# A two-layer streaming encoder on one core: pooling mixer by halves of 512 columns, its bands and cached tokens parked in DRAM ahead, and running sums of log f formed with the projections

## The chip, the cores and the metric

One core of one Trainium2 chip runs the whole program as a single launch. The metric is device time in microseconds (us). Engines are called PE (TensorE), DVE (VectorE), ACT (ScalarE), POOL (GpSimd) and SP (SyncE); SP issues nearly all of this kernel's DMAs, in the order in which they stand in its queue. All data are float32 at the interface. Every large product is made from three single-pass products of a high and a low part (`hi`, `lo`, `xh`, `xl`, `uh`, `ul`): `hi` is the rounded copy (`fp32r`) and `lo` the rest.

## What is computed

One inference step of two layers over 1,152 tokens: 1,024 of a new prompt, and 16 new tokens of each of 8 running streams. Model width 1,024, feed-forward width 2,816.

- Layer 0's mixer: one projection gives q, f, i, g of a gated linear recurrence (HGRN, 4 heads of 128) and q, k, v of a differential attention (4 heads), which runs over the prompt and over 2,048 cached tokens of each stream; an output projection follows.
- Layer 1's mixer pools the last 2, 4, 8 or 16 rows per group of 256 channels, with 15 cached rows for each stream, and multiplies each group by its 256x256 weight.
- Each mixer is followed by a layer norm, a feed-forward block with a convolution over three rows (ConvFFN), and a layer norm.

The recurrence, and the pooling, which the change touches:

```python
def hgrn2_chunk(S0, q, log_f, k, v):
    b = jnp.cumsum(log_f, axis=1)
    decay = jnp.where(causal, jnp.exp(jnp.minimum(b[:, :, None] - b[:, None, :], 0.0)), 0.0)
    scores = jnp.einsum('bthk,btshk,bshk->bhts', q, decay, k)
    o = einsum('bhts,bshv->bthv', scores, v) + einsum('bthk,bhkv->bthv', q * jnp.exp(b), S0)
    S = S0 * jnp.exp(b[:, -1])[..., None] + einsum('bshk,bshv->bhkv', k * jnp.exp(b[:, -1:] - b), v)

def mixer_pool(x, pos0, hist, w_groups, scale):
    xh = jnp.concatenate([hist, x], axis=1)
    cs = jnp.cumsum(jnp.pad(xh, ((0, 0), (1, 0), (0, 0))), axis=1)
    for g, w in enumerate((2, 4, 8, 16)):
        s = cs[:, 16:, sl] - cs[:, 16 - w:16 - w + T, sl]
        outs.append((s / minimum(w, pos + 1) - x[..., sl]) @ w_groups[g])
    return jnp.concatenate(outs, axis=-1) * scale, xh[:, -15:]
```

## The kernel before

The tokens are nine tiles of 128 rows: tiles 0 to 7 the prompt, tile 8 the streams (`NPT = 8`, `NT = 9`). A tile framework reorders instructions over the engines by priority, and gives buffers by tag; an instruction that writes into a tag whose buffers are all in use waits until one is free. The stages around the change, in the order of the program:

1. **Projections.** `fm_group` (L369) makes q, k and log f for each of the four heads with features on partitions, 128 x 1,152, and stores them to the DRAM scratch `fm_scr` (`out_fm`, L385). The last DVE step for log f is the subtraction at L401; its store stands in SP's queue among the loads `kraw` and `vraw` of cached keys and values. This stage is woven with the attention of the streams over their cached tokens.
2. **HGRN** (`hgrn`, L803). Nine blocks of 128 tokens in two lanes: the stream block (8), 1, 3, 5, 7 and 0, 2, 4, 6. For m = 1, 2, 4, ..., 64 (four levels for the stream block) `level_prep` makes one level: with tokens in pairs of runs of m, `qk` holds q times the decay from the pair's middle in the second run, and k times the decay up to it in the first. Two running tiles are kept for this, `P` (sums of log f from the start of a run to the token) and `sf` (from the token to the run's end). Each level ends with DVE adding a run's total onto the next one, in place, for `sf` (L847) and `P` (L849), on half of the 512 columns; the first level copies and clears `sf` (L842, L843). So the next level's exponentials (ACT) come after this level's sums. `put` multiplies `qk` on PE and copies the scores under a mask (L861, L873). When all levels are through, `edge_prep` makes `qb` and `kb` (L894, L895) for the state's part, and `outputs` or `outputs_streams` the products with v and the state S. Attention of the remaining streams is woven in, and gives PE other work.
3. **ConvFFN of layer 0.** The second product runs by groups of two of the 22 feature blocks; a group is nine tiles of twelve matmuls `pd`, and DVE adds each into `acc` (L1471). Weights come through `raw` (3 buffers) and are cast into `wh`, `wl` (8 buffers each), a group ahead.
4. **Pooling mixer** (`pool_mixer`, L1575). At its start SP loads two thirds of the window matrices (`band`, 128 x 128 for each term and channel group) into `raw` and DVE casts them (L1553). For each tile n, `project` multiplies the tile by the scaled pool weights into PSUM `pu` (24 matmuls of 256 columns) and splits it into `uh`, `ul` (128 x 1,024, 3 buffers each); `windows(n-1)` applies the band matrices to tiles n-1 and n-2 (`py`, 16 matmuls), adds into `acc` (L278), and starts the layer norm; `to_xt` transposes an older tile (`pxt`) for the next block. At n = 4, `bring_history` loads the 120 cached rows (`hist`), transposes them (`ph`, 8 on PE), splits them into `hh`, `hl`, and the last two band matrices are loaded and cast.

```python
            for n in range(NT + 1):
                if n == 4:
                    bring_history()
                    band_s = load_bands(pw, 3, 2)
```

Helpers: L144 issues a matmul, L153 a transpose, L156/L157 the split into a high part (ACT) and a low part (DVE or POOL), L278 the residual addition, L243 to L249 the layer norm's last steps.

Of the kernel before, what the change touches and what calls it, by code (L numbers as in the profile page):

```python
# [111 lines left out]
def hybrid_stream_kernel(ctx: ExitStack, tc: tile.TileContext, i, o, k):  # L112
# [198 lines left out]
    t4_scr = [dr.tile([4, 2, 128, NTOK // 2], F32, name=f"t4_scr{l}") for l in range(2)]  # L311
    g_scr = [dr.tile([NF, 128, NTOK], F32, name=f"g_scr{l}") for l in range(2)]
# [56 lines left out]
    def fm_group(st, c0, which):  # L369
        wh, wl = load_cols(w_in, c0)  # L370
        for j in range(2):
# [29 lines left out]
            nc.vector.tensor_tensor(lf, z, lf, ALU.subtract)  # L401
            out_fm(lf, 1)
# [397 lines left out]
    def hgrn(hg, hc, fm0, v0, before_last):  # L800
# [13 lines left out]
        def begin(bi):  # L814
# [10 lines left out]
            blk[bi] = dict(q=fm[0], P=fm[1], k=fm[2], v=v, sf=sf, sc=sc)  # L825

        def level_prep(bi, mi):
            B = blk[bi]
            q, P, kf, sf = B["q"], B["P"], B["k"], B["sf"]
            m = LEVELS[mi]  # L830
            g = 512 // (2 * m)
# [51 lines left out]
        def edge_prep(bi):  # L883
# [4 lines left out]
            nc.scalar.activation(kb, B["sf"], AF.Exp)  # L888
# [549 lines left out]
    def ffn_down(l, last, ahead):  # L1438
# [108 lines left out]
    def load_bands(pool, j0, n):  # L1547
        band = pool.tile([128, n, 4, 128], F32R, name=f"band{j0}")
        for j in range(0, n, 2):
            m = min(2, n - j)  # L1550
# [22 lines left out]
    def pool_mixer(acc, late, ws):  # L1573

        with ExitStack() as ph:  # L1575
            pw = pool_of(ph, "wpl", 1)
            band = load_bands(pw, 0, 3)
# [10 lines left out]
            def bring_history():  # L1588
                hist = raw_tile("hist")
                nc.sync.dma_start(hist[0:120, :], i["state_pool"][0].rearrange("b j d -> (b j) d"))  # L1590
                for j in range(0, KD, 4):
                    p = bank([128, 4, 120], "ph")
                    for q in range(4):
                        tr(p[:, q, :], hist[0:120, (j + q) * 128:(j + q + 1) * 128], 120)
                    split(hh[:, j:j + 4], hl[:, j:j + 4], p)

            def project(fh, fl, n):
                uh = sp.tile([n, D], F32R, tag="uh", name="uh", bufs=3)
                ul = sp.tile([n, D], F32R, tag="ul", name="ul", bufs=3)
                for j in range(2):  # L1600
                    p = bank([n, 2, 256], "pu")
                    for gg in range(2):
# [101 lines left out]
```

## Time and profile before

| | us |
|---|---|
| three timed runs | 2553.20, 2555.87, 2557.08 (median 2555.87) |
| the profiled execution | 2553.18 |
| its span, first to last instruction | 2551.2 |
| PE busy | 2487.2 (97%) |
| DVE, ACT, POOL busy | 1509.5 (59%), 1069.5 (42%), 954.6 (37%) |
| mean granted clock of PE | 0.988 of full speed |

Times in the trace count from the span's start. "Busy" is the time in which an engine has an instruction in hand. A list of waits names, for each engine, the line that waited and the line or DMA that released it. A table by stretch gives busy time for each engine between two points, with the clock granted to PE, as a fraction of 2.4 GHz. Stages by time: projections with cached-token attention up to about 585, HGRN from there to about 760, the first ConvFFN up to about 1660, the pooling mixer from about 1640 to 1762, the second ConvFFN after it.

### The profile page before, as it was taken

How to read it: one execution, taken by the hardware profiler on the slowest of the kernel's cores; microseconds unless marked ns; L12 is line 12 of the kernel's file. 1: busy time of each engine (PE TensorE's matmuls, PEld its weight loads, DVE VectorE, ACT ScalarE, POOL GpSimd, SP SyncE). 2: the span in 40 equal slices, each digit the busy share in tenths (PEclk: the TensorE clock that was granted, in tenths of full speed). 3: DMA queues.
4: the chain of work that ended last, by engine and by line, in shares of the span. 5: the costliest groups of instructions: out<-in, count | busy, mean ns of one | idle time of the engine just before them, and what ended most of it. 6: DMA issues, size and time to landing. Idle time of an engine off the chain costs nothing.

```text
span 2551.2 us, 45246 instructions
## 1 busy us (share of the span) xinstructions
PE 2487.2 (97%) x18042; PEld 2305.0 (90%) x18042; DVE 1509.5 (59%) x2652; ACT 1069.5 (42%) x2167; POOL 954.6 (37%) x726
## 2 busy tenths in 40 slices
PE   8999999998999999999999999969999999999998
PEld 8999998886879999999999788869999999987886
DVE  3377754348984484555555655777655555556557
ACT  3255555354772544444444121266344444431114
POOL 1110111006642555555554122244455555531214
PEclk9999999998999999999999999989999999999999
DMA  5634337787866214222224322223232222252222
GB/s 181 193 107 132 95 129 244 241 268 240 255 200 243 98 55 148 78 78 70 71 78 172 125 97 80 78 62 108 98 115 78 78 70 70 78 210 96 84 92 84
DMA packets 279250, 323.78 MB, mean 127 GB/s; under 512 B 46347, under 2 KB 209748, under 8 KB 279039
## 3 DMA queue, kind: packets, MB, share of 16 engines
q1 hardware_dynamic: 276613, 319.26, 38.6%
q8 instruction: 142, 2.33, 0.4%
q10 hardware_dynamic: 2426, 1.63, 0.3%
q14 instruction: 69, 0.57, 0.1%
HBM read 244.38 MB, written 76.46 MB: 126 GB/s over the span
## 4 chain that ended last, share of the span: by engine, by line
PE 64%; DVE 2%; ACT 2%; issue 1%; DMA 1%; POOL 0%; DVEq 0%; SPq 0%; ACTq 0%; POOLq 0%
PE pu L144 39%; PE pd L144 20%; PE po L144 4%; DVE acc L243 1%; PE pxt L153 1%; ACT junk_ln L237 1%; ACT acc L244 0%; DMA graw<-g_scr 0%; DVE xl L157 0%; DVE acc L278 0%; DVE gl L157 0%; DMA raw<-in_ffn_w_up 0%; DMA hist<-in_state_pool 0%; PE pc L153 0%; POOL acc L249 0%
## 5 line engine op out<-in xcount | busy, mean ns | idle before, releaser
L157 POOL TENSOR_TENSOR lo<-raw,hi 128x512 fp32r<-128x512 f32 x360 | 514.6, 1443 | 1086.7 <-ACT hi L156 963.8
L144 PE MATMUL pu<-xl,hi 128*128 128x288 f32 (+1 forms) x1536 | 469.6, 306 | 2.8 <-DVE xl L157 2.8
L144 PE MATMUL pu<-xh,hi 128*128 128x288 f32 (+1 forms) x1536 | 470.4, 306 | 0.0
L144 PE MATMUL pu<-xh,lo 128*128 128x288 f32 (+1 forms) x1536 | 469.6, 306 | 0.0
L156 ACT CAST hi<-raw 128x512 fp32r<-128x512 f32 x376 | 229.0, 620 | 530.3 <-PE pu L144 263.3
L144 PE MATMUL pd<-lo,gh 128*128 128x512 f32 x792 | 315.4, 398 | 0.0
L144 PE MATMUL pd<-hi,gh 128*128 128x512 f32 x792 | 314.8, 398 | 0.3 <-ACT gh L156 0.2
L144 PE MATMUL pd<-hi,gl 128*128 128x512 f32 x792 | 310.4, 393 | 0.4 <-DVE gl L157 0.4
L144 PEld LDWEIGHTS pu<-xl,hi 128*128 128x128 f32 x1536 | 289.8, 189 | 3.1 <-DVE xl L157 3.1
L144 PEld LDWEIGHTS pu<-xh,lo 128*128 128x128 f32 x1536 | 289.6, 189 | 0.0
L144 PEld LDWEIGHTS pu<-xh,hi 128*128 128x128 f32 x1536 | 289.5, 189 | 0.0
L1471 DVE TENSOR_TENSOR acc<-acc,pd 128x512 f32<-128x512 f32 x324 | 212.7, 682 | 118.7 <-PE pd L144 118.3
L144 PE MATMUL ptm<-hi,xh 128*128 128x256 f32 x720 | 209.7, 291 | 0.0
L144 PE MATMUL ptm<-hi,xl 128*128 128x256 f32 x720 | 202.3, 281 | 1.3 <-DVE xl L157 1.3
L144 PE MATMUL ptm<-lo,xh 128*128 128x256 f32 x720 | 202.0, 281 | 0.0
L1243 DVE SCALAR_TENSOR_TENSOR cv<-ext,prm,cv 128x1024 f32<-128x1024 f32 (+1 forms) x176 | 183.9, 1098 | 21.9 <-ACT cv L1240 21.9
L144 PEld LDWEIGHTS pd<-hi,gh 128*128 128x128 f32 x792 | 149.0, 188 | 38.4 <-ACT gh L156 1.2
L144 PEld LDWEIGHTS pd<-hi,gl 128*128 128x128 f32 x792 | 148.8, 188 | 37.2 <-DVE gl L157 1.3
L144 PEld LDWEIGHTS pd<-lo,gh 128*128 128x128 f32 x792 | 149.0, 188 | 33.7
L144 PEld LDWEIGHTS ptm<-hi,xh 128*128 128x128 f32 x720 | 136.7, 190 | 2.1 <-issue 1.0
L144 PEld LDWEIGHTS ptm<-hi,xl 128*128 128x128 f32 x720 | 136.3, 189 | 1.6 <-DVE xl L157 1.6
L144 PEld LDWEIGHTS ptm<-lo,xh 128*128 128x128 f32 x720 | 136.7, 190 | 0.4
(332 smaller groups left out, 5645.0 us busy)
## 6 DMA issues: line engine op xcount, KB each, us to landing
raw<-in_ffn_w_up SPq DMA_DIRECT2D x88, 512.0 KB
kraw<-in_cache_k SPq DMA_DIRECT2D x64, 512.0 KB
vraw<-in_cache_v SPq DMA_DIRECT2D x64, 512.0 KB
g_scr<-cv SPq DMA_DIRECT2D x44, 576.0 KB
graw<-g_scr SPq DMA_DIRECT2D x44, 576.0 KB
raw<-in_ffn_w_down SPq DMA_DIRECT2D x44, 512.0 KB
raw<-in_w_in_ab SPq DMA_DIRECT2D x28, 512.0 KB
x_scr<-acc SPq DMA_DIRECT2D x18, 512.0 KB
```

Source lines behind the costliest of these rows:

```text
L144: nc.tensor.matmul(out, a, b, start=start, stop=stop, skip_group_check=True)
L153: nc.tensor.matmul(out, in_, ident[:n, :n], is_transpose=True)
L156: nc.scalar.copy(hi, src)
L157: (sub or nc.vector).tensor_tensor(lo, src, hi, ALU.subtract)
L237: nc.scalar.activation(junk_ln, acc_t, AF.Square, bias=st[:, 0:1], accum_out=st[:, 1:2])
L243: nc.vector.scalar_tensor_tensor(acc_t, acc_t, st[:, 0:1], g_bc, ALU.add, ALU.mult)
L1243: nc.vector.scalar_tensor_tensor(dst, tap[j], cw[j], dst, ALU.mult, ALU.add)
L1471: nc.vector.tensor_tensor(acc[t][:, cs], acc[t][:, cs], p, ALU.add)
```

## The change

Three parts.

**Running sums.** `fm_group` turns log f in place into running sums from the start of each block of 128 tokens (of each 16 for the streams): seven DVE additions a head for m = 1, ..., 64 ahead of the store. In `hgrn`, `level_prep` no longer updates `P` and `sf`; one DVE subtraction (`sums_from`) gives both runs' differences from the pair's middle in a tile `d` (three buffers), and ACT's exponential of the first run takes it with scale -1. No level needs another, and `edge_prep`, with a subtraction of its own, none of them.

**Pooling by halves.** `project` and `windows` work on 512 columns at a time, `uh` and `ul` are 512 columns wide with 7 buffers each, and the second half of `windows(n-2)` stands between the two halves of `project(n)`.

**Parking.** While layer 0's second product runs, at group 4 the cached rows are loaded, transposed, split and stored to `h_scr`, at group 5 the five band matrices are loaded, cast and stored to `b_scr`. The pooling mixer loads the finished tiles.

```diff
@@ hybrid_stream_kernel: DRAM scratch
+    b_scr = dr.tile([5, 128, 512], F32, name="b_scr")
+    h_scr = dr.tile([2, 2, 128, 480], F32, name="h_scr")
@@ fm_group, after log f of a head
             nc.vector.tensor_tensor(lf, z, lf, ALU.subtract)
+
+            for m in LEVELS:
+                v = lf[:, 0:NTOK if m < 16 else SEQ].rearrange("p (b two j) -> p b two j", two=2, j=m)
+                nc.vector.tensor_tensor(v[:, :, 1, :], v[:, :, 1, :],
+                                        v[:, :, 0, m - 1:m].to_broadcast([128, v.shape[1], m]), ALU.add)
             out_fm(lf, 1)
@@ hgrn: begin
-            sf = hg.tile([128, H, 128], F32, tag="sf", name="sf", bufs=3)
...
@@ hgrn: level_prep
-            vq, vP, vs = v2(qk), v2(P), v2(sf)
-            nc.scalar.activation(vq[:, :, 1, :], vP[:, :, 1, :], AF.Exp)
+            vq, vd = v2(qk), sums_from(P, 2 * m, m - 1, m == 1).rearrange("p b (two j) -> p b two j", two=2)
+            nc.scalar.activation(vq[:, :, 1, :], vd[:, :, 1, :], AF.Exp)
             nc.gpsimd.tensor_tensor(vq[:, :, 1, :], vq[:, :, 1, :], v2(q)[:, :, 1, :], ALU.mult)
             if m == 1:
                 nc.vector.tensor_copy(vq[:, :, 0, :], v2(kf)[:, :, 0, :])
-                nc.vector.memset(vs[:, :, 1, :], 0.0)
-                nc.vector.tensor_copy(vs[:, :, 0, :], vP[:, :, 1, :])
             else:
-                nc.scalar.activation(vq[:, :, 0, :], vs[:, :, 0, :], AF.Exp)
+                nc.scalar.activation(vq[:, :, 0, :], vd[:, :, 0, :], AF.Exp, scale=-1.0)
                 nc.gpsimd.tensor_tensor(vq[:, :, 0, :], vq[:, :, 0, :], v2(kf)[:, :, 0, :], ALU.mult)
-                nc.vector.tensor_tensor(vs[:, :, 0, :], vs[:, :, 0, :],
-                                        vP[:, :, 1, m - 1:m].to_broadcast([128, g, m]), ALU.add)
-            nc.vector.tensor_tensor(vP[:, :, 1, :], vP[:, :, 1, :],
-                                    vP[:, :, 0, m - 1:m].to_broadcast([128, g, m]), ALU.add)
             B["qk", mi] = qk
+
+        def sums_from(P, w, at, second=False):
+
+            d = hg.tile([128, H, 128], F32, tag="sf", name="d", bufs=3)
+            dv, pv = [x.rearrange("p h (b j) -> p (h b) j", j=w) for x in (d, P)]
+            r = slice(w // 2 if second else 0, w)
+            nc.vector.tensor_tensor(dv[:, :, r], pv[:, :, r],
+                                    pv[:, :, at:at + 1].to_broadcast([128, 512 // w, r.stop - r.start]), ALU.subtract)
+            return dv
@@ hgrn: edge_prep
-            nc.scalar.activation(kb, B["sf"], AF.Exp)
+            w = 16 if bi == NPT else 128
+            nc.scalar.activation(kb.rearrange("p h (b j) -> p (h b) j", j=w), sums_from(B["P"], w, w - 1), AF.Exp, scale=-1.0)
@@ conv_ffn: loop over the down groups
+                if n == 4 and t == 0 and not last:
+                    park_history()
+                if n == 5 and t == 0 and not last:
+                    park_bands()
@@ pool mixer helpers
-    def load_bands(pool, j0, n):
...
+    def load_band(pool, j, tag):
+        band = pool.tile([128, 4, 128], F32R, tag=tag, name="band", bufs=1)
+        nc.sync.dma_start(band.rearrange("p g t -> p (g t)").bitcast(F32), b_scr[j])
+        return band
+
+    def park_bands():
+
+        for j in range(0, 5, 2):
+            m = min(2, 5 - j)
             raw = raw_tile()
-            nc.sync.dma_start(raw[:, 0:512 * m], k["band"][:, j0 + j:j0 + j + m].rearrange("p a g t -> p (a g t)"))
-            nc.vector.tensor_copy(band[:, j:j + m].rearrange("p a g t -> p (a g t)"), raw[:, 0:512 * m])
-        return band
+            nc.sync.dma_start(raw[:, 0:512 * m], k["band"][:, j:j + m].rearrange("p a g t -> p (a g t)"))
+            for q in range(m):
+                b = wp.tile([128, 512], F32R, tag="wh", name="b", bufs=8)
+                nc.vector.tensor_copy(b, raw[:, 512 * q:512 * q + 512])
+                nc.sync.dma_start(b_scr[j + q], b.bitcast(F32))
+
+    def park_history():
+
+        hist = raw_tile("hist")
+        nc.sync.dma_start(hist[0:120, :], i["state_pool"][0].rearrange("b j d -> (b j) d"))
+        for j in range(0, KD, 4):
+            p = bank([128, 4, 120], "ph")
+            for q in range(4):
+                tr(p[:, q, :], hist[0:120, (j + q) * 128:(j + q + 1) * 128], 120)
+            parts = [wp.tile([128, 512], F32R, tag=t, name=n, bufs=8) for t, n in (("wh", "hh"), ("wl", "hl"))]
+            split(*[x[:, 0:480] for x in parts], p.rearrange("p q t -> p (q t)"))
+            for n in range(2):
+                nc.sync.dma_start(h_scr[n, j // 4], parts[n][:, 0:480].bitcast(F32))
@@ pool_mixer
-            band = load_bands(pw, 0, 3)
+            band = [load_band(pw, j, f"b{j}") for j in range(3)]
...
-            def bring_history():
...
-            def project(fh, fl, n):
...
+            def project(fh, fl, n, m, j):
+                p = bank([m, 2, 256], "pu")
+                for gg in range(2):
+                    g = 2 * j + gg
+                    for kk in range(2):
+                        f = 2 * g + kk
+                        mm3(p[:, gg, :], fh[:, f, :], fl[:, f, :], ws[g][0][kk], ws[g][1][kk], kk == 0, kk == 1)
+                us[n, j] = [sp.tile([m, 512], F32R, tag=t, name=t, bufs=7) for t in ("uh", "ul")]
+                split(*us[n, j], p.rearrange("p g c -> p (g c)"))
+
+            def project_tile(n, j):
+                if n == NPT:
+                    project(hh, hl, n, 120, j)
+                else:
+                    a = min(n, NPT) * 128
+                    project(xh[:, :, a:a + 128], xl[:, :, a:a + 128], n, 128, j)
-            def windows(t, terms):
...
+            def windows(t, j):
+
...
+                    terms = [(band[0], us[0, j])]
+                elif t < NPT:
+                    terms = [(band[1], us[t, j]), (band[2], us[t - 1, j])]
+                else:
+                    terms = [(band_s[0], us[NT, j]), (band_s[1][0:120], us[NPT, j])]
...
+            band_s = []
+            for n in range(NPT + 1):
+                if n == 3:
+                    band_s += [load_band(pw, 3, "b0"), load_band(pw, 4, "b3")]
+                    for x, h in ((hh, h_scr[0]), (hl, h_scr[1])):
+                        nc.sync.dma_start(x.rearrange("p (a q) t -> p a (q t)", a=2).bitcast(F32),
+                                          h.rearrange("a p t -> p a t"))
                 if n == 6:
                     first = [load_up(1, 0, nc.vector), load_up(1, FF, nc.vector)]
-                if n == NPT:
-                    us[n] = project(hh, hl, 120)
-                else:
-                    a = min(n, NPT) * 128
-                    us[n] = project(xh[:, :, a:a + 128], xl[:, :, a:a + 128], 128)
+                project_tile(n, 0)
+                if n > 1:
+                    windows(n - 2, 1)
+                project_tile(n, 1)
                 ln_apply()
                 if n == 0:
                     nc.sync.dma_start(o["pool_p"][0, 0], acc[NPT - 1][128 - HIST:128, :])
                 if late and n < 3:
                     t = late.pop(0)
                     to_xt(acc[t], t * 128)
-                if n == 1:
-                    windows(0, [(band[:, 0], us[0])])
-                elif 1 < n <= NPT:
-                    windows(n - 1, [(band[:, 1], us[n - 1]), (band[:, 2], us[n - 2])])
+                if n == NPT:
+                    project_tile(NT, 0)
+                if n:
+                    windows(n - 1, 0)
                 if n > LATE_UP:
                     to_xt(acc[n - 1 - LATE_UP], (n - 1 - LATE_UP) * 128)
-            windows(NPT, [(band_s[:, 0], us[NT]), (band_s[0:120, 1], us[NPT])])
+            project_tile(NT, 1)
+            windows(NPT - 1, 1)
+            to_xt(acc[NPT - LATE_UP], (NPT - LATE_UP) * 128)
+            windows(NPT, 0)
+            ln_apply()
+            windows(NPT, 1)
```

On DVE, at the start of HGRN. `fm_7246` holds q and log f, `fm_7247` k and v of the stream block before; `fm_7276` and `fm_7277` the same in the change; `fm` is a prompt block's. Before:

```order
L842 MEMSET sf 128x256
L849 TENSOR_TENSOR fm_7246<-fm_7246 128x256
L951 TENSOR_TENSOR vb<-fm_7247,vmask 128x512
L873 COPY_PREDICATED sc<-masks,psc 128x256
L841 COPY qk<-fm 128x256
L843 COPY sf<-fm 128x256
L849 TENSOR_TENSOR fm<-fm 128x256
L861 COPY_PREDICATED sc<-masks,psc 128x512
L847 TENSOR_TENSOR sf<-sf,fm_7246 128x128x2
L847 TENSOR_TENSOR sf<-sf,fm 128x128x2
L849 TENSOR_TENSOR fm_7246<-fm_7246 128x128x2
```

and in the change:

```order
L857 TENSOR_TENSOR d<-fm_7276 128x256
L846 COPY qk<-fm_7277 128x256
L960 TENSOR_TENSOR vb<-fm_7277,vmask 128x512
L869 COPY_PREDICATED sc<-masks,psc 128x512
L900 COPY fl<-qb 128x32
L904 TENSOR_TENSOR qb<-qb,fm_7276 128x512
L881 COPY_PREDICATED sc<-masks,psc 128x256
L947 COPY qe<-qb 128x4x16
L948 COPY qe<-qb 128x4x16
L947 COPY qe<-qb 128x4x16
L948 COPY qe<-qb 128x4x16
L857 TENSOR_TENSOR d<-fm 128x256
```

One subtraction into `d` stands for two additions, and the stream block's `qb` and `qe`, which stood behind all its levels, now stand ahead of the second one.

On SP, at the start of the pooling mixer, ending with the cached rows (`acc_16453`, `acc_16446` are tiles of the residual). Before:

```order
L1563 DMA raw<-in_pool_w 128x4x256
L1552 DMA raw<-const_band 128x1024
L1552 DMA raw<-const_band 128x512
L1648 DMA out_pool_p<-acc_16453 15x1024
L282 DMA g_bc<-in_ln_g 128x1024
L1581 DMA b_bc<-in_ln_b 128x1024
L1583 DMA rc<-const_rcnt 128x4
L1650 DMA out_pool_s<-acc_16454 15x1024 x8
L257 DMA x_scr_95<-acc_16446 128x1024
L1590 DMA hist<-in_state_pool 120x1024
```

and in the change:

```order
L1614 DMA b_bc<-in_ln_b 128x1024
L171 DMA raw<-in_ffn_w_up 128x8x128
L1688 DMA out_pool_p<-acc_16483 15x1024
L171 DMA raw<-in_ffn_w_up 128x8x128
L1562 DMA band<-b_scr 128x512 x3
L282 DMA g_bc<-in_ln_g 128x1024
L1616 DMA rc<-const_rcnt 128x4
L1690 DMA out_pool_s<-acc_16484 15x1024 x8
L1562 DMA band<-b_scr 128x512 x2
L1678 DMA hh<-h_scr 128x2x480
L1678 DMA hl<-h_scr 128x2x480
L257 DMA x_scr_95<-acc_16476 128x1024
```

The finished history tiles stand ahead of the first store of a normalised tile (`x_scr`), where the raw rows stood behind it; the first bands stand behind two loads of feed-forward weights and a store of pooled rows.

On PE, in the second product of the first ConvFFN, the rows around the transposes of the cached rows in the change; before, they stood between `py` and `pu` of the pooling mixer:

```order
L144 MATMUL pd<-hi,gh 128x512
L144 MATMUL pd<-lo,gh 128x512
L144 MATMUL pd<-hi,gl 128x512
L153 MATMUL ph<-ident,hist 128x120 x8
L144 MATMUL pd<-hi,gh 128x512
L144 MATMUL pd<-lo,gh 128x512
```

## Rows read from the trace of the kernel before

**Rows 1.** The page: busy time and share of each engine, and the chain that ended last.

```profile
PE 2487.2 (97%) x18042; PEld 2305.0 (90%) x18042; DVE 1509.5 (59%) x2652; ACT 1069.5 (42%) x2167; POOL 954.6 (37%) x726
...
PE 64%; DVE 2%; ACT 2%; issue 1%; DMA 1%; POOL 0%; DVEq 0%; SPq 0%; ACTq 0%; POOLq 0%
```

**Rows 2.** Waits of PE, whole span: line waited for, us in total, times, longest.

```profile
PE ph L153 <- DMA hist<-in_state_pool: 9.4, 1, 9.4
...
PE po L946 <- DVE qe L938: 5.3, 2, 2.9
PE py L144 <- DVE band L1553: 5.2, 1, 5.2
...
PE psc L144 <- DVE S L924: 2.4, 3, 1.3
PE psc L144 <- POOL qk L839: 2.2, 1, 2.2
...
PE pS L144 <- DVE vb L951: 1.6, 1, 1.6
PE py L144 <- ACT uh L156: 1.5, 1, 1.5
```

**Rows 3.** Chain that ended last, pooling mixer: start us, us, what.

```profile
1695.14 3.93 DMA b_bc<-in_ln_b
...
1712.85 5.34 DMA hist<-in_state_pool
...
1718.32 1.83 PE ph L153 x8
```

**Rows 4.** Pooling mixer by stretch: us, busy (instructions) of each engine, clock, DMA.

```profile
1681.00:1698.00 17.00, 10.23 (x77) 9.62 (x76) 15.96 (x25) 10.90 (x19) 7.11 (x3) 0.83 0.22 67
1698.00:1762.00 64.00, 52.13 (x405) 50.77 (x404) 46.32 (x108) 41.33 (x74) 26.56 (x13) 0.91 0.36 118
1718.40:1725.00 6.60, 6.60 (x40) 6.60 (x41) 4.19 (x5) 2.30 (x4) 5.20 (x3) 0.66 0.27 110
```

**Rows 5.** DVE in 1698:1762, groups by form: count, busy us, mean ns, idle before.

```profile
L1553 DVE CAST band<-raw 128x1024 fp32r<-128x1024 f32 x1 | 2.3, 2269 | 4.8 <-DMA raw<-const_band 4.8
L157 DVE TENSOR_TENSOR hl<-ph,hh 128x480 fp32r<-128x480 f32 x2 | 1.2, 643 | 0.0
```

**Rows 6.** HGRN by stretch, columns as in rows 4.

```profile
613.00:640.00 27.00, 20.04 (x151) 11.65 (x151) 25.59 (x69) 9.89 (x20) 13.53 (x17) 0.81 0.71 206
660.00:700.00 40.00, 38.20 (x457) 34.31 (x456) 39.71 (x76) 31.82 (x92) 28.73 (x35) 1.00 0.79 247
```

**Rows 7.** DVE in 560:760, groups by form.

```profile
L849 DVE TENSOR_TENSOR fm<-fm 128x256 f32<-128x256 f32 x60 | 39.6, 668 | 0.9 <-ACT qk L838 0.3
L847 DVE TENSOR_TENSOR sf<-sf,fm 128x256 f32<-128x256 f32 x51 | 38.2, 759 | 0.7 <-ACT qk L845 0.6
...
L894 DVE TENSOR_TENSOR kb<-kb,fm 128x512 f32<-128x512 f32 x9 | 7.8, 864 | 0.6 <-ACT kb L888 0.6
...
L843 DVE COPY sf<-fm 128x256 f32<-128x256 f32 x9 | 4.2, 471 | 0.0
...
L842 DVE MEMSET sf<- 128x256 f32 x9 | 2.4, 272 | 0.0
```

**Rows 8.** DVE's timeline in HGRN, two single instructions: start us, us, what.

```profile
597.13 0.41 DVE L847 TENSOR_TENSOR sf<-sf,fm 128x256 f32<-128x256 f32 x1
...
620.85 0.68 DVE L951 TENSOR_TENSOR vb<-fm,vmask 128x512 f32<-128x512 f32 x1
```

**Rows 9.** Projections with cached-token attention, by stretch, columns as in rows 4.

```profile
390.00:566.00 176.00, 176.00 (x1763) 152.45 (x1756) 70.57 (x128) 89.34 (x132) 18.83 (x14) 1.00 0.78 248
```

**Rows 10.** DVE, whole span: an addition of 128x576 in the ConvFFN.

```profile
L1302 DVE TENSOR_TENSOR sb<-sc,sb 128x576 f32<-128x576 f32 x8 | 6.0, 755 | 0.3
```

**Rows 11.** Waits of SP's queue in 390:566, as rows 2.

```profile
SPq L688 <- PE pos L703: 55.8, 23, 4.0
...
SPq L386 <- DVE lf L401: 11.9, 3, 5.0
```

More of the change, by code (lines that the diff above doesn't have):

```diff
@@ L821, in begin @@
                 fm = [fm[:, w] for w in range(3)]
-            sf = hg.tile([128, H, 128], F32, tag="sf", name="sf", bufs=3)
             sc = hg.tile([128, H, 128], F32, tag="sc", name="sc", bufs=3)
             nc.gpsimd.memset(sc, 0.0)
-            blk[bi] = dict(q=fm[0], P=fm[1], k=fm[2], v=v, sf=sf, sc=sc)
+            blk[bi] = dict(q=fm[0], P=fm[1], k=fm[2], v=v, sc=sc)
         def level_prep(bi, mi):
             B = blk[bi]
-            q, P, kf, sf = B["q"], B["P"], B["k"], B["sf"]
+            q, P, kf = B["q"], B["P"], B["k"]
             m = LEVELS[mi]
-            g = 512 // (2 * m)
             def v2(x):
@@ L1586, in pool_mixer @@
             hl = pw.tile([128, KD, 120], F32R, name="hl")
-            def bring_history():
[L1589 to L1595, printed above, removed]
@@ L1597, in project @@
-            def project(fh, fl, n):
[L1598 to L1602, printed above, removed]
-                        g = 2 * j + gg
-                        for kk in range(2):
-                            f = 2 * g + kk
-                            mm3(p[:, gg, :], fh[:, f, :], fl[:, f, :], ws[g][0][kk], ws[g][1][kk], kk == 0, kk == 1)
-                    cs = slice(512 * j, 512 * j + 512)
-                    split(uh[:, cs], ul[:, cs], p.rearrange("p g c -> p (g c)"))
-                return uh, ul
@@ L1611, in windows @@
-            def windows(t, terms):
-                sums = sp.tile([128, 4], F32, tag="sums", name="sums")
-                if t == 0:
-                    nc.scalar.mul(acc[t], acc[t], ALPHA)
-                for j in range(2):
-                    p = bank([128, 2, 256], "py")
-                    for gg in range(2):
-                        g = 2 * j + gg
-                        cs = slice(256 * g, 256 * g + 256)
-                        n = 0
-                        for bm, us in terms:
-                            for u in us:
-                                mm(p[:, gg, :], bm[:, g, :], u[:, cs], n == 0, n == 2 * len(terms) - 1)
-                                n += 1
-                        if t == 0:
-                            nc.vector.scalar_tensor_tensor(acc[t][:, cs], p[:, gg, :], rc[:, g:g + 1], acc[t][:, cs],
-                                                           ALU.mult, ALU.add, accum_out=sums[:, g:g + 1])
-                    if t:
-                        add_res(acc[t], slice(512 * j, 512 * j + 512), p.rearrange("p g c -> p (g c)"),
-                                sums[:, j:j + 1])
-                layer_norm(sp, acc[t], sums if t == 0 else sums[:, 0:2], g_bc, b_bc, nc.gpsimd if t in PG else None, scr_rows(1, t))
@@ L1634, in pool_mixer @@
-            us = {}
-            for n in range(NT + 1):
-                if n == 4:
-                    bring_history()
-                    band_s = load_bands(pw, 3, 2)
+            us = {}
+            def project(fh, fl, n, m, j):
[7 more added lines that the diff above has]
+                split(*us[n, j], p.rearrange("p g c -> p (g c)"))
@@ new lines, in project_tile @@
+            def project_tile(n, j):
[4 more added lines that the diff above has]
+                    project(xh[:, :, a:a + 128], xl[:, :, a:a + 128], n, 128, j)
+            all_sums = {}
+            def windows(t, j):
+                if j == 0:
+                    all_sums[t] = sp.tile([128, 4], F32, tag="sums", name="sums")
+                sums = all_sums[t]
+                if t == 0:
+                    if j == 0:
+                        nc.scalar.mul(acc[t], acc[t], ALPHA)
+                    terms = [(band[0], us[0, j])]
[3 more added lines that the diff above has]
+                    terms = [(band_s[0], us[NT, j]), (band_s[1][0:120], us[NPT, j])]
+                p = bank([128, 2, 256], "py")
+                for gg in range(2):
+                    g = 2 * j + gg
+                    cs = slice(256 * g, 256 * g + 256)
+                    n = 0
+                    for bm, hl2 in terms:
+                        for u in hl2:
+                            mm(p[:, gg, :], bm[:, g, :], u[:, 256 * gg:256 * gg + 256], n == 0, n == 2 * len(terms) - 1)
+                            n += 1
+                    if t == 0:
+                        nc.vector.scalar_tensor_tensor(acc[t][:, cs], p[:, gg, :], rc[:, g:g + 1], acc[t][:, cs],
+                                                       ALU.mult, ALU.add, accum_out=sums[:, g:g + 1])
+                if t:
+                    add_res(acc[t], slice(512 * j, 512 * j + 512), p.rearrange("p g c -> p (g c)"), sums[:, j:j + 1])
+                if j == 0:
+                    return
+                layer_norm(sp, acc[t], sums if t == 0 else sums[:, 0:2], g_bc, b_bc, nc.gpsimd if t in PG else None, scr_rows(1, t))
```

3 lines of the change are left out of this document (removed).

## The prediction

> **What bounds the kernel.** I read the page first. PE is busy for 97% of the span and makes up 64% of the chain that ended last; no other engine passes 59% [rows 1]. The span is 2551.2 us, so PE is without work for 2551.2 - 2487.2 = 64 us in all. The change adds no matmul and takes none away, so it can only win from those 64 us, and from stretches in which PE was given less than its full clock. The list of PE's waits says where the idle time lies [rows 2]: the largest single wait, 9.4 us, is for the load of the cached rows in the pooling mixer; 5.2 us more for the cast of the window matrices there; in HGRN two waits for `qe` (5.3), three for the state S (2.4), one for `qk` (2.2) and one for `vb` (1.6). The tables by stretch then show what stands behind the waits. In HGRN, DVE is busy for 39.71 of 40 us in one stretch and 25.59 of 27 in another [rows 6], so the waits on DVE there are for a full engine. In the pooling mixer PE's clock is 0.83 and 0.66 around the two gaps [rows 4]. In the projections PE has no gap in 176 us [rows 9]; nothing can be won there, only lost.
>
> **The pooling mixer.** The cached rows are issued at 1712.85 and land 5.34 us later [rows 3]; SP reaches them only behind the store of a normalised tile. PE stands for 9.4 us [rows 2], transposes for 1.83 us at a reduced clock [rows 3], and in the 6.6 us from there on runs at 0.66 of its clock [rows 4], which costs 6.6 x 0.34 = 2.2 us, 1.83 x 0.34 = 0.6 of it in the transposes. In the change the finished tiles are issued at tile 3, ahead of that store, and used five tiles later: gap, transposes and the remaining 1.6 us of clock go: 9.4 + 1.8 + 1.6 = 12.8 us. The transposes return in the feed-forward block at full clock, 1.83 x 0.66 = 1.2 us. The rest of the parking costs nothing that I can see on PE: five casts and two splits on DVE, busy for 59% of the span [rows 1], and some loads and stores on SP's queue, beside `pd` matmuls whose weights are cast a group ahead. If that cover were gone, the eight `wh` buffers that the casts share would hold up weights, and PE would wait for them by the microsecond.
>
> The first window matrices wait for a cast now, 5.2 us [rows 2]. In the change they come by DMA without one, but stand on SP behind two weight loads and a store of pooled rows. The nearest row for such a load is the bias vector, 3.93 us from issue to landing [rows 3]; issued near 1690, the first lands near 1694, against 1695.8 for PE's start before. I take 3.5 us of the gap as staying, so 1.7 are won; between 0 and 5.2. The clock of 0.83 over 10.23 busy us costs 1.7 us [rows 4]; a gap two thirds as long gives 0.5 back.
>
> At the end, products by halves let PE start on the first 512 columns while the second are being split: of the wait for `uh`, 1.5 us [rows 2], 1.2 goes. Against this, with the gaps closed DVE has less room. From 1698 to 1762 it is busy for 46.32 us [rows 4], less 2.3 for the cast and 1.2 for the split [rows 5], so 42.8; PE's 52.13, less 3.4 for the transposes and the clock, is 48.7. PE still sets the pace, but DVE at 88% in order will hold it now and then: plus 2 us, between 0 and 5.
>
> Pool sum: -12.8 + 1.2 - 1.7 - 0.5 - 1.2 + 2 = -13 us; ends -18 and -6.
>
> **HGRN.** Removed from DVE: 60 and 51 additions on 256 columns, nine copies, nine clears, 39.6 + 38.2 + 4.2 + 2.4 = 84.4 us [rows 7]. Added: 60 subtractions on 512 columns (51 in levels, 9 for the edges) and 9 on 256. The nearest row for 512 columns in this stage is the multiplication for `kb`, also with two operands in SBUF, 0.864 us [rows 7]; with 0.668 for 256 columns that is 60 x 0.864 + 9 x 0.668 = 57.9 us. DVE wins 26 us. The other end: alone, 256 columns take 0.41 us and 512 take 0.68 [rows 8]. If the rest of the 0.668 and 0.759 is time shared with POOL that follows the columns and not the instructions, removed and added must both be counted by these: 111 x 0.41 + 4.2 + 2.4 = 52.1 against 60 x 0.68 + 9 x 0.41 = 44.5, and only 8 us are won. I take 26, since the 0.864 was measured beside the same POOL work.
>
> The Trainium skill ("VectorE: DVE Perf Modes", Mode 1× (REGULAR) — the baseline) says that such an operation gives one result per cycle, whatever its shape, so the number of columns would count and not that of instructions. By that rule only the fixed part of 60 instructions would go, some 8 us of DVE. The lone instructions agree, 0.27 us more for 256 columns more, or 1.05 ns a column [rows 8]; the stage's means, 0.668 and 0.864, do not.
>
> What DVE wins is not what PE wins: PE only has its waits to give. Those for `qk` (2.2) and the first loads stay, since the first level still goes through DVE, ACT and POOL. The two for `qe`, 5.3 us, come because the copies stand behind all levels of the stream block and behind one long reduction; in the change's order they stand early, and I leave 1.5. For S 2.4 becomes 1.2, for `vb` 1.6 becomes 0.8. The clock of 0.81 over 20.04 busy us in 613 to 640 costs 3.8 us [rows 6]; with the gaps there mostly gone half returns. Sum: -3.8 - 1.2 - 0.8 - 1.9 = -7.7 us, say -8; ends 0 (ACT, busy for 31.82 of 40 us [rows 6], takes DVE's place) and -16 (all those waits and the clock, and some waits too small for the list's head).
>
> **Projections.** 28 additions on 512 or 576 columns: by 0.755 us [rows 10] 21 us more on DVE, which has 70.57 of 176 us busy [rows 9]. They stand between copies out of PSUM one at a time, so a copy comes at most one addition later. Streams go on between the last head's store and HGRN's first load. 0 us; upper end +4.
>
> **Sum.** -13 - 8 + 0 = -21 us on the profiled execution, 2553.18, which gives 2532.2. The median of the runs shown, 2555.87, is 2.7 above that execution, so I predict 2535 us. A measurement of this kernel tells about 0.2%, 5.1 us, from no change.
>
> **Rivals.**
> - *DVE saves only the fixed part* (the second price above, 8 us). The waits for `qe` still shrink by the new order, the others stay: HGRN -3, total -16, 2540. For it: removed and added work have the same columns, 111 x 256 + 18 x 256 = 60 x 512 + 9 x 256, and the list of 256-column rows has a lone 0.41. Against: the same stage's `kb` row at 0.864 for twice the columns of 0.759. Chance 0.15.
> - *The pooling mixer becomes bound elsewhere.* The tiles or the first bands land late because SP sits behind the pooled rows' stores and weight loads, or DVE, 42.8 us in what would then be about 50, holds PE at each tile: pool -5, HGRN -6, 2545. Chance 0.15.
> - *The store of running sums holds up SP.* In 390 to 566, SP already waits 11.9 us in three pieces for log f [rows 11], with loads of cached keys and values queued behind it. Seven additions of 0.755 put among other DVE work make the store some 6 to 10 us later, four times. If the loads ahead do not cover that, PE starves each time, 6 us and 2 for the clock: 4 x 8 = 32 us, total +11, 2567. Slower than before from about 27 us of such waits on. For it: DMA's share of 0.78 there [rows 9]. Against: SP's largest wait there, 55.8 us, is for buffers that PE has yet to free [rows 11], so loads are ahead of use; and PE has not one gap in the stretch. Chance 0.06.
> - *The change does not do what it says.* Parked tiles and weights compete for the eight buffers, and the weights of three groups come 6 us late each: -21 + 18, so 2553. For it: the parked parts take buffers of the tags that weights use. Against: no wait of `pd` for weights stands among PE's longer ones [rows 2]. Chance 0.06.
> The forecast itself has 0.58.
>
> **How the numbers follow.** Faster by more than 0.2% (below 2550.8): the forecast, the first rival and nearly all of the second, 0.87. Within 0.2%: a little of the second and the fourth, 0.07. Slower: 0.06. The ends of the terms give 2556 - 18 - 16 = 2522 and 2556 - 6 - 0 + 4 = 2554; all at one end at once is unlikely. From 2520 to 2547 holds the forecast with its bounds and the first two rivals for the most part, and leaves out the others.
>
> **What would show it.** Right: no wait of `ph`; the first `py` waits for a band's DMA by 3 to 4 us; PE's clock at 1.00 from there to the mixer's end; in HGRN DVE's share falls from 99% to 85% or less, `d` on 512 columns near 0.86 us, and `qe` gone from the head of PE's waits; no gap of PE before 566. Wrong: `d` near 1.1 us or more, so that DVE is as full as before; PE waiting for `hh`, `uh` or `acc` in the mixer; `pd` waiting for weights near groups 4 to 6; PE waiting for `kraw` or `vraw` behind a store of `lf`.

## The result and the profile after

The change runs at 2534.59 us (median of four; 2533.34 to 2537.41) against 2555.55 for the kernel before (median of four): a ratio of 0.9919, 95% interval 0.9907 to 0.9931. The profiled execution took 2534.15 us, its span is 2532.2, so 19.0 us shorter than before's. The page's lines for engines and for the chain, which answer to [rows 1]:

```profile
PE 2479.9 (98%) x18042; PEld 2301.2 (91%) x18042; DVE 1513.4 (60%) x2622; ACT 1068.5 (42%) x2167; POOL 965.9 (38%) x726
...
PE 91%; DVE 4%; DMA 2%; ACT 2%; issue 1%; POOL 0%; SPq 0%; ACTq 0%; DVEq 0%; POOLq 0%
```

PE is idle for 52 us now, where it was 64. The two chains can't be compared by their shares: those of before add up to 70% of the span, those of the change to 100%. PE's busy time fell by 7 us too, with the same instructions: they ran at a higher clock or were held up less.

Where the time went is best seen by stages. I took the start of the first or last instruction of a kind on PE from the timelines: projections from the first to the last `pfm`, HGRN from the first `psc` to the last `pS`, the output projection from there to the last transpose of `ot`, the first ConvFFN from its first `pu` to its last `pd`, the mixer from there to the last `py`.

| us | projections | HGRN | output projection | first ConvFFN | mixer |
|---|---|---|---|---|---|
| before | 175.4 | 168.6 | 54.6 | 799.1 | 77.8 |
| the change | 178.7 | 157.4 | 56.3 | 799.3 | 63.9 |
| difference | +3.3 | -11.2 | +1.7 | +0.2 | -13.9 |

The stretches between these differ by less than 0.1 us, except 0.8 us more ahead of the projections; all together make the 19.0.

PE's waits, whole span, as [rows 2]:

```profile
PE pxt L153 <- POOL acc L249: 5.3, 5, 1.9
PE py L144 <- DMA band<-b_scr: 4.2, 1, 4.2
...
PE psc L144 <- DMA fm<-fm_scr: 2.3, 1, 2.3
PE pS L144 <- DVE qe L947: 2.3, 1, 2.3
PE po L955 <- DMA s<-in_state_hgrn: 2.1, 2, 1.9
PE psc L144 <- POOL qk L844: 2.0, 1, 2.0
PE pfm L144 <- ACT pT L692: 1.9, 1, 1.9
...
PE pS L144 <- DVE fl L902: 1.1, 1, 1.1
PE psc L144 <- DVE S L933: 0.7, 2, 0.5
...
PE py L144 <- ACT uh L156: 0.4, 1, 0.4
PE py L144 <- DVE ul L157: 0.4, 1, 0.4
```

The wait of `ph` is gone. That of `py` for the cast, 5.2, became one for a band's DMA, 4.2. In HGRN the waits for `vb` are gone and those for S are a third; those for `qe`, 5.3 us, have 2.3 + 1.1 + 2.1 us for `qe`, `fl` and the loaded state in their place. The wait for the first block's load grew from 1.2 to 2.3. A new one stands in the projections, 1.9 us.

DVE in HGRN (560 to 750 us, by form), as [rows 7], then POOL there:

```profile
L857 DVE TENSOR_TENSOR d<-fm 128x512 f32<-128x512 f32 x60 | 56.8, 973 | 0.3 <-ACT qk L843 0.3
...
L903 DVE TENSOR_TENSOR kb<-kb,fm 128x512 f32<-128x512 f32 x9 | 8.4, 929 | 0.6 <-ACT kb L897 0.6
...
L857 DVE TENSOR_TENSOR d<-fm 128x256 f32<-128x256 f32 x9 | 5.4, 605 | 1.2 <-DMA fm<-fm_scr 1.2
```

```profile
L844 POOL TENSOR_TENSOR qk<-qk,fm 128x256 f32<-128x256 f32 x60 | 59.8, 1000 | 29.1 <-ACT qk L843 26.1 <-PE ppt L153 2.8
L849 POOL TENSOR_TENSOR qk<-qk,fm 128x256 f32<-128x256 f32 x51 | 51.0, 1000 | 0.1
```

DVE was relieved of 84.4 us and got 62.2; POOL's own products grew from 100.7 to 110.8 us. The mean of 0.973 us for `d` on 512 columns is made of two kinds: 11 of the 60 have POOL idle beside them for most of their time and take 0.69 us, 44 have it busy for most of it and take 1.05. The additions of before on 256 columns took 0.41 to 0.43 and 0.75 to 0.83 us in these two cases. So beside a busy POOL an instruction took 0.3 to 0.4 us longer, on 512 columns as on 256. The Trainium skill ("SBUF — State Buffer", Who interferes with whom) says that a DVE instruction with two inputs in SBUF and a GpSimd one that reads SBUF contend for one port, which one of them holds alone; that both engines' instructions got longer agrees with it.

HGRN and the mixer by stretch, columns as in [rows 4, 6]:

```profile
613.00:640.00 27.00, 21.51 (x229) 13.83 (x228) 21.12 (x61) 13.12 (x35) 13.92 (x18) 1.00 0.72 222
...
660.00:700.00 40.00, 39.47 (x469) 35.96 (x472) 37.52 (x62) 32.74 (x96) 34.56 (x38) 1.00 0.77 257
```

```profile
1692.00:1738.80 46.80, 46.08 (x374) 45.67 (x374) 39.16 (x90) 33.41 (x60) 24.97 (x11) 0.95 0.45 147
1691.00:1695.00 4.00, 3.79 (x18) 3.83 (x19) 2.65 (x5) 1.27 (x3) 0.30 (x1) 0.50 0.92 298
```

In the mixer PE works almost without a break from 1692 on, DVE at 84%; the clock is still 0.50 for some 4 us behind the first `py`'s wait.

### The profile page after: what moved, and what is told of

It reads as the page before. It is cut to its first block, busy times and chain, and to the rows that moved or that the text cites. A ratio compares the mean times of both kernels' runs of the same rounds, so it can differ in the third digit from the quotient of the medians.

```text
span 2532.2 us, 45250 instructions
## 1 busy us (share of the span) xinstructions
PE 2479.9 (98%) x18042; PEld 2301.2 (91%) x18042; DVE 1513.4 (60%) x2622; ACT 1068.5 (42%) x2167; POOL 965.9 (38%) x726
## 4 chain that ended last, share of the span: by engine, by line
PE 91%; DVE 4%; DMA 2%; ACT 2%; issue 1%; POOL 0%; SPq 0%; ACTq 0%; DVEq 0%; POOLq 0%
PE pu L144 40%; PE pd L144 20%; PE ptm L144 10%; PE po L144 6%; PE pfm L144 3%; PE pk L153 2%; PE psc L144 2%; PE s L144 1%; PE pxt L153 1%; PE pss L659 1%; PE pos L710 1%; DVE acc L243 1%; PE pat L153 1%; PE py L144 1%; PE ppt L153 0%
```

## The experiments

Theory: the mixer's gain is the parking's, and HGRN's is the waits on a full DVE, most of that through the stream block's `qe`. Rivals: the halves are needed for the first; the order alone, or DVE's time alone, makes the second. Each group of four (e1 to e4, e5 to e8, e9 to e12) shared one chip, with before at a median of 2555.7 to 2556.0 in each.

**Each part alone: e1, e2, e3.** The three parts of the diff, one at a time, on the kernel before (in e2 `bring_history` and `load_bands` stay; in e3 `project` and `windows` do).

e1:

```diff
             nc.vector.tensor_tensor(lf, z, lf, ALU.subtract)
+            for m in LEVELS:
...
-            vq, vP, vs = v2(qk), v2(P), v2(sf)
+            vq, vd = v2(qk), sums_from(P, 2 * m, m - 1, m == 1)...
```

e2, with 6 buffers for each of `uh`, `ul`:

```diff
-            def project(fh, fl, n):
+            def project(fh, fl, n, m, j):
...
-            def windows(t, terms):
+            def windows(t, j):
```

e3:

```diff
+                if n == 4 and t == 0 and not last:
+                    park_history()
...
-            band = load_bands(pw, 0, 3)
+            band = [load_band(pw, j, f"b{j}") for j in range(3)]
```

> The kernel before with the running sums alone (projections and HGRN), pooling mixer as it was. If the parts add up by stage: projections 3 to 4 us longer than before, HGRN (first psc to last pS) 157 us against 168.5, pooling mixer 78 us as before, total 5 to 8 us below before (about 2548 to 2551). Rival, that HGRN's shorter time in the changed kernel came from elsewhere: HGRN within 3 us of 168.5 and the total equal to before or above it by the projections' loss.

> The kernel before with the pooling mixer by halves of 512 columns (6 buffers for each of uh and ul, where the change has 7, since the bands and the cached rows are still loaded raw and cast in the mixer). If the parking carries the mixer's gain: the wait of ph stays at 8 to 10 us, that of py for the cast at about 5, the waits for uh and ul at the end shrink from 2.5 to about 0.7; mixer 75 to 77 us against 77.8, total 1 to 3 us below before. Rival, that the order by halves lets PE work through the wait for the cached rows: ph's wait below 5 us and the mixer below 72.

> The kernel before with the parking alone, project and windows on whole tiles. If the parking carries the mixer's gain by itself: no wait of ph, py's first wait for a band's DMA about 4 us, mixer 65 to 67 us against 77.8 before and 63.9 in the change, total 10 to 12.5 us below before. Rival, that whole tiles leave PE waiting for uh and ul once the gap is gone, and the halves are needed: mixer 68 us or more, with waits of py for uh or ul of 3 us and more in all.

| | median us (lowest to highest) | ratio, 95% interval | projections | HGRN | mixer |
|---|---|---|---|---|---|
| e1 sums | 2549.49 (2545.99 to 2558.23) | 0.9983 (0.9971 to 0.9994) | 179.1 | 156.1 | 78.0 |
| e2 halves | 2550.59 (2548.95 to 2553.58) | 0.9981 (0.9972 to 0.9990) | 175.9 | 169.2 | 73.6 |
| e3 parking | 2541.69 (2541.44 to 2542.13) | 0.9943 (0.9928 to 0.9958) | 175.4 | 169.6 | 63.1 |

HGRN's gain and the projections' loss come with the sums, the mixer's with the parking: 63.1 us without the halves is no more than the change's 63.9. Halves alone won 4 us of mixer and 5.4 of the median where I had expected 1 to 3, with the wait of `ph` unchanged; parking alone won 14.3 us of the median where I had expected 10 to 12.5. Each row's stages are those of one execution, and e1's was the fastest of ten. PE's waits in e2, then e3:

```profile
PE ph L153 <- DMA hist<-in_state_pool: 9.6, 1, 9.6
```

```profile
PE py L144 <- DMA band<-b_scr: 4.5, 1, 4.5
...
PE py L144 <- DVE ul L157: 1.0, 2, 0.6
```

**Order or time in HGRN: e4, e5.** e4 puts the stream block's `qb` behind all its levels again; e5 doubles the subtraction at three levels (and the stream block's one for the edge), 27 more instructions, and keeps the order.

```diff
 def edge_prep(bi):
+    if bi == NPT:
+        nc.vector.tensor_copy(B["P"][:, :, 0:1], B["P"][:, :, 0:1])
```

```diff
 def sums_from(P, w, at, second=False):
...
+    if not second and w in (4, 16, 64):
+        nc.vector.tensor_tensor(dv[:, :, r], pv[:, :, r], ..., ALU.subtract)
```

> The changed kernel with one added copy of a column of P onto itself for the stream block (0.15 us on DVE), so that its qb, and with it qe, again comes behind the last of that block's subtractions. If HGRN's 11 us come mainly from the early qe: the waits for qe or for what follows from it return, 4 to 6 us, and HGRN becomes 161 to 164 us long against 157.4, total 3 to 6 us above the change. Rival, that they come from DVE's shorter time: HGRN 157 to 159, total within 1.5 us of the change.

> The changed kernel with the subtraction for three of the seven levels (m = 2, 8, 32) done twice into the same tile: 26 more instructions on 512 columns, by 0.97 us in the changed kernel's trace some 25 us more on DVE in HGRN, as much as the change took from it, with the new order kept. If DVE's time is worth only what is left after the order (2.8 us in the run with the late edge): HGRN 158 to 161 us against 157.4, total 0 to 3 us above the change. Rival, that DVE's time is worth most of HGRN's gain: HGRN 163 us or more, total 6 us or more above the change.

e4: 2540.02 us (2536.87 to 2543.78), HGRN 165.7. e5: 2553.35 us (2550.05 to 2558.51), HGRN 175.2. Taken alone, e4's 165.7 says that the order makes the gain. The trace does not bear that out, once HGRN is split into PE's idle time, the time that the clock cost (PE's busy time times one minus the granted clock, over stretches of 3 us) and the rest:

| HGRN, us | idle | clock | rest | sum |
|---|---|---|---|---|
| before | 15.2 | 9.9 | 143.5 | 168.6 |
| the change | 11.3 | 6.1 | 140.0 | 157.4 |
| e1, the same HGRN | 9.4 | 6.2 | 140.4 | 156.1 |
| e4, late edge | 11.0 | 13.3 | 141.4 | 165.7 |
| e5, DVE's time put back | 19.7 | 11.8 | 143.7 | 175.2 |
| e7 (below), HGRN as in the change | 8.7 | 13.1 | 140.6 | 162.4 |

e7 has the change's HGRN, instruction for instruction, and loses 13.1 us by the clock where the change lost 6.1. So the clock's part differs from one execution to the next, and e4 differs from the change by little else: 0.3 us less idle, 1.4 more of the rest. In both e4 and e7 it is a low clock behind the first loads that lasts on, here in e4, then e7, with PE busy throughout:

```profile
612.00:622.00 10.00, 10.00 (x64) 9.01 (x63) 6.30 (x13) 3.83 (x9) 2.31 (x2) 0.50 0.36 101
```

```profile
611.00:621.00 10.00, 10.00 (x64) 9.01 (x63) 4.61 (x10) 3.70 (x10) 2.30 (x3) 0.50 0.30 95
```

This rests on one execution of e4. Its median is 5.4 us above the change's, which was not run beside it, and inside the 3 to 6 us that the order's reading had set, and its other executions have no trace; that the order is worth nothing in them is not shown.

e5 brings back before's rest and more than its idle time. DVE is busy for 160 us of HGRN there, 155 before and 138 in the change, so it puts back somewhat more than was taken; and since the second subtraction stands ahead of its own level's exponentials, it does not separate DVE's total time from a longer way through three levels. Its first waits are mostly for DVE:

```profile
PE pS L144 <- DVE vb L963: 4.2, 3, 2.4
PE psc L144 <- POOL qk L849: 4.1, 4, 2.0
PE psc L144 <- DVE S L936: 3.9, 3, 1.7
```

**The projections: e6.** The seven additions on POOL.

```diff
-                nc.vector.tensor_tensor(v[:, :, 1, :], v[:, :, 1, :],
+                nc.gpsimd.tensor_tensor(v[:, :, 1, :], v[:, :, 1, :],
```

> The changed kernel with the 28 running-sum additions of the projections on POOL in place of DVE. If DVE's added 24 us make the 3.3 us that the projections lost: first to last pfm 175.4 us as before instead of 178.7, no gap of PE before HGRN, total 2 to 4 us below the change. Rivals: the loss is the longer chain to the store of log f and not DVE's time (POOL takes 1.0 us for 256 columns in HGRN, so a head's seven additions some 15 us): first to last pfm stays at 178 or grows; or POOL's work slows DVE's copies and the projections lose more than 3.3.

2542.01 us (2533.52 to 2546.05), projections 180.1, and 4 us more between them and HGRN. The projections lost more, not less, as both rivals had it; of the two the trace shows the longer way to the store. In the change's timeline (DVE, ACT, PE; start, us, idle before and its releaser) the attention's maximum `mx` comes behind the additions, its exponential late on ACT, and behind that and six more instructions of ACT the copy `pT` on which PE waits:

```profile
437.85 1.57 DVE L407 TENSOR_TENSOR lf<-lf 128x512 f32<-128x512 f32 x1
...
439.55 1.56 DVE L407 TENSOR_TENSOR lf<-lf 128x512 f32<-128x512 f32 x1
...
441.30 2.30 DVE L676 TENSOR_REDUCE mx<-Sx 128x1 f32<-128x2064 f32 x1
```

```profile
443.64 2.02 ACT L678 ACTIVATE Sx<-Sx,mx 128x2064 f32<-128x2064 f32 x1 [2.94 <-DVE mx L676]
...
451.09 0.35 ACT L692 COPY pT<-ppt 128x256 f32<-128x256 f32 x1
```

```profile
451.49 0.45 PE L144 MATMUL pfm<-xh,hi 128*128 128x384 f32 x1 [1.88 <-ACT pT L692]
```

In e6 the maximum comes earlier, but ACT stands for the store of the sums: `ks` of the next head shares the one buffer of tag `lf`. DVE, then ACT:

```profile
437.69 2.30 DVE L676 TENSOR_REDUCE mx<-Sx 128x1 f32<-128x2064 f32 x1
```

```profile
446.12 1.28 ACT L395 ACT_TABLE_LOAD   x1 [2.53 <-DMA fm_scr<-lf]
```

**The halves and the first band: e7, e8, and again e9 to e12.** e7 is the change without the halves. e8 takes the bands from a pool at the other end of SBUF, e12 adds a longer lag in HGRN. e9 is the change itself; e9 to e12 shared one chip.

```diff
+            pb = pool_of(ph, "bpl", 1, side="right")
-            band = [load_band(pw, j, f"b{j}") for j in range(3)]
+            band = [load_band(pb, j, f"b{j}") for j in range(3)]
```

```diff
-        LAG = 4
+        LAG = 5
```

> The change without the halves: running sums and parking, project and windows on whole tiles. If the halves give nothing once the cached rows and bands are parked: mixer 63 to 64.5 us against 63.9 in the change, total within 2 us of the change. Rival, that the halves carry part of the mixer's gain beside the parking: mixer 66 us or more, total 2 to 5 us above the change.

> The changed kernel with the band tiles in a pool at the other end of SBUF, over tiles that are free when the feed-forward block's last pd is done, so that their loads stand on SP ahead of the two weight loads and the store of pooled rows. If the first bands are late because of their place in the queue and their tiles' space: py's first wait of 4.2 us goes and the low clock behind it (0.50 for 4 us), mixer 58 to 60 us against 63.9, total 4 to 6 us below the change. Rival, that the next thing is late as well (bias vector, weights for the next block, layer norm of the last tiles): the wait moves to another operand of py or pxt and the mixer stays above 62.

> The change itself, on one chip beside the next three, so that they can be compared with it: 2533 to 2540 us, PE's mean granted clock 0.990 to 0.993, the spread between executions by that clock (0.001 is some 2.5 us).

> Running sums and parking without the halves, as in e7, beside the change. In e7's trace the mixer was 2.3 us shorter than the change's, HGRN with the same instructions 5 us longer by PE's clock alone. If the halves give nothing beside the parking: median within 2.5 us of the change. Rival, that e7's 2542 us was the halves' worth: 4 us or more above the change again.

> The band tiles at the other end of SBUF, as in e8, beside the change. In e8's trace the mixer was 6.7 us shorter than the change's (57.2 against 63.9), while three of its four executions were at a clock of 0.990 to 0.991. If the gain stands: median 3 to 6 us below the change. Rival, that the earlier loads cost elsewhere what they win: within 1.5 us of the change.

> As e11, and in HGRN the score products follow the levels' preparation by five steps in place of four, so that products of the streams' attention stand between the first ones, where PE waits 2.0 us for qk and 1.6 to 2.3 for the first block's load and then runs at 0.50 of its clock. If those two waits start the low clock: they shrink below 2 us together, the clock's loss in HGRN falls from 6 to 13 us to 4 or less, total 4 to 8 us below e11. Rival, that the waits move a step on with the products (table load and DMA come first in any case): HGRN 156 to 162 us as before, total within 2 us of e11.

| | median us (lowest to highest) | HGRN | of it clock | mixer |
|---|---|---|---|---|
| e7 sums and parking | 2542.29 (2539.84 to 2543.02) | 162.4 | 13.1 | 61.7 |
| e8 bands on the right | 2535.76 (2526.99 to 2536.62) | 157.2 | 7.3 | 57.3 |
| e9 the change | 2532.80 (2532.38 to 2533.34) | 157.2 | 7.3 | 62.0 |
| e10 as e7 | 2536.90 (2534.73 to 2541.27) | 157.0 | 7.4 | 63.3 |
| e11 as e8 | 2530.22 (2528.95 to 2537.52) | 162.2 | 12.6 | 57.3 |
| e12 bands and lag | 2533.05 (2531.42 to 2534.06) | 160.4 | 7.8 | 61.0 |

*Halves.* In the traces the mixer without them takes 63.1 (e3), 61.7 and 63.3 us, with them 63.9 and 62.0: nothing. Yet the medians of e7 and e10 lie 7.7 us (not run beside it) and 4.1 us (beside it) above the change's, so e10 met its rival's condition of 4 us or more, and each of its five executions is slower than each of e9's four. For e7 the profiled execution lost 7 us by the clock in HGRN. For e10, whose profiled execution is only 2 us slower than e9's, the mixer is 1.3 and the first ConvFFN 2.0 us longer, and neither is more than these stages differ by among the other traces. What the halves are worth beside the parking stays open, between nothing and some 4 us.

*The first band.* The change's SP queue shows why it is late (start, us of the issues):

```profile
1667.44 0.38 SPq L171 DMA_DIRECT2D raw<-in_ffn_w_up  x1
1685.88 0.36 SPq L1688 DMA_DIRECT2D out_pool_p<-acc  x1
1686.47 0.38 SPq L171 DMA_DIRECT2D raw<-in_ffn_w_up  x1
1686.90 2.30 SPq L1562 DMA_DIRECT2D band<-b_scr  x3
```

The bands stand behind the store of pooled rows, and PE goes on 4.3 us after their issue. In e9 the same wait, 4.4 us, is put down to a cast on ACT; there too it ends 4.5 us after the bands' issue. In e8 four of them are issued from 1644.69 on (the edit moves their place in the queue by way of their place in SBUF, and does not tell the two apart), and PE's only waits in the mixer are these:

```profile
PE py L144 <- ACT uh L156: 2.0, 2, 1.4
PE pxt L153 <- POOL acc L249: 1.1, 1, 1.1
PE py L144 <- DVE ul L157: 0.5, 2, 0.4
```

The mixer is 57.3 us in both runs, and the clock costs nothing in it; in e12, with the same bands, it is 61.0: the band's wait is gone there too, but PE waits 2.9 us for `acc`, and the clock costs 1.7. The median of e8 is 1.2 us above the change's first one, where 4 to 6 below was expected. That of e11, 2.6 us below e9's where 3 to 6 was expected, is the lowest of all kernels here; but its interval against before, 0.9892 to 0.9919, overlaps the change's, 0.9896 to 0.9923. So the gain is shown in the mixer and not in the medians. e12's wait for the first block's load went, others came (`vb` 2.2, S 2.0), as its rival had it; its median is 2.8 us above e11's, a little outside the 2 us of that rival.

## Why the prediction was right

Forecast 2535 us, measured 2534.6; the range held. By its steps:

- **The mixer with the transposes, -13 us, measured -13.9 + 0.2 = -13.7.** The wait of `ph` and the transposes went whole. The first band came 4.2 us late where I left 3.5, for the reason given, its place on SP. The tail gave a little more: `uh` went from 1.5 to 0.4 us, and `ul`, which I had not counted, from 1.0 to 0.4. The clock gave back less: 3.9 us lost in the mixer before (same reckoning as in HGRN's table), 2.9 after, since it is still at 0.50 behind the first wait; "PE's clock at 1.00 from there" failed. The 2 us for a crowded DVE did not come as such; PE waited for POOL's `acc` instead, 2.9 us in the mixer in place of 1.6. That the halves carry part of the tail's 1.2 us is not shown: e3 has the same mixer without them. The ends, -18 and -6, are not what the bounds of the terms give (-18.5 and -8.3); nothing hangs on that.
- **The transposes in the ConvFFN, +1.2 of that sum.** The stage grew by 0.2 us, and in traces of one kernel it differs by up to 1.6 us (e8, e11); a cost of the parking there can't be seen, and one of 1 us can't be ruled out.
- **HGRN, -8 us, measured -11.2, and for another reason than the largest item.** "DVE wins 26 us" was close: `d` took 0.973 us where I set 0.864, so 22 us, and the first rival's 8 us is out. By the Trainium skill's rule of one result per cycle ("VectorE: DVE Perf Modes", Mode 1× (REGULAR) — the baseline) DVE would have won no more than those 8 us; what decided are the 0.3 to 0.4 us more that an instruction took beside a busy POOL, whatever its columns. The step that failed is "the two for `qe` ... I leave 1.5": in place of 5.3 us PE waited 5.5 for the early `qe`, for `fl` and for the state, and in e4's trace putting `qe` late again costs 1 us beside the clock. What e5 shows in its place is DVE's time: 3.9 us of idle time at many small waits where I had summed 5.8, and 3.5 us of what the profile counts as busy, which I had excluded with "PE only has its waits to give"; what held PE inside its busy time stays open. DVE's share did not fall "to 85% or less" everywhere: in 660 to 700 it went from 99% to 94%, so it was still nearly full. The other 3.8 us are the clock, against 1.9 forecast: the low clock of 613 to 640, 0.81 before, is gone whole, where I let half of it return. In e8, e9 and e10 some 1.7 us of it are back, and in e4, e7 and e11 the low clock behind the first loads costs about 12 us in place of 6, with no edit that would explain it in e7 and e11; that the profiled execution had neither is partly luck.
- **The projections, 0 with +4 as the end, measured +3.3.** The additions took 23.6 us where I set 21. I looked for late copies out of PSUM; what came late was a reduction and, through ACT, the copy behind it, so "no gap of PE before 566" failed. The rival of a held SP queue did not occur: no load is among PE's waits before HGRN.
- **The output projection, +1.7,** was not in the sum; it returned some of HGRN's gain: the clock cost 2.9 us there, 1.7 before.

So the total was met by errors of both signs. On the profiled executions -19.0 us stand against -21: 3.2 more from HGRN and 0.7 from the mixer, 3.3, 1.7 and 0.8 us lost in the projections, behind HGRN and ahead of the projections. The medians differ by 21.0.

## What to carry to other kernels

A stall on a DMA behind a long queue was worth its wait plus the clock behind it here, and moving its preparation into a stage with cover gave nearly the whole sum; look then at the next load in the same queue, which was 4 us. On an engine that is full, price the instructions by rows measured beside the same neighbours, and do not credit the gain to the one wait at the list's head: take the order and the time apart by experiment. Split a stage into idle time, clock and the rest before comparing two traces of it, and do not take one trace for the kernel: here one stage of one code differed by 6 us.

## What was not expected of the hardware

The same instructions of HGRN, after the same two waits, ran at the low clock for different lengths of time. PE in 610 to 620 us of e9, then of e11, whose HGRN is the same and starts 1 us earlier:

```profile
610.00:620.00 10.00, 10.00 (x127) 7.63 (x126) 7.78 (x19) 4.36 (x13) 7.94 (x12) 1.00 0.40 117
```

```profile
610.00:620.00 10.00, 10.00 (x66) 9.18 (x60) 3.69 (x9) 4.66 (x13) 3.50 (x5) 0.52 0.15 53
```

Both had waited 2.0 us for `qk` and 1.8 to 2.0 for a load near 590; one was back at 2.4 GHz by 610, the other ran at 1.2 GHz on to nearly 620, with PE busy for all of the 10 us in both. That is 5 us of HGRN between these two traces. Whole executions follow the mean clock too: of e11's, two at 0.993 took 2529 us and one at 0.990 took 2537.5. Those have no trace, so where they lost it is not shown; the traced one, at 0.991, took 2531.
